# Light expert steps that fold gate and up apart, and a first gather whose second one-hot comes ahead of the splits

## Chip, core and metric

One core of a Trainium2 chip runs the whole program. The time is device time in microseconds (us) from the runs of the compiled program; the trace is one execution by the hardware profiler. Engines: PE is TensorE (matmuls), PEld its weight loads, DVE VectorE, ACT ScalarE, SP the queue that issues nearly all DMAs.

## What is computed

A two-layer decoder trunk on 256 tokens of width 1024, in float32. The first layer is FoX attention and a dense SwiGLU, the second a Griffin recurrent block and a mixture of eight SwiGLU experts, of which each token uses two. After each channel mixer a gated per-layer embedding is added. The change lies in the experts:

```python
def _moe_swiglu(x, w_router, b_router, w_gu, w_down):        # cut
    logits = xt @ w_router + b_router
    top_logit, top_idx = lax.top_k(logits, 2)
    top_w = softmax(top_logit)
    # tokens sorted by expert, and for each expert e:
    gate, up = split(xs @ w_gu[e], 2)                        # (n, 1024) @ (1024, 2 * 3584)
    y = (silu(gate) * up) @ w_down[e]                        # (n, 3584) @ (3584, 1024)
    out = zeros.at[row_tok].add(y * row_w)
```

## The kernel before

Every float32 matrix is cut into two parts of reduced precision, `hi` (a cast on ACT, L131) and `lo` (the rest, a subtraction on DVE, L132); a product is the sum of hi-hi, hi-lo and lo-hi matmuls. The weights are streamed: the class `Stream` holds a list of 1 MiB chunks, loads them ahead on SP's queue into whatever room is free, and splits them, two pieces to a chunk. Split pieces lie in four buffers each for `whi` and `wlo`, so a split can run only as far ahead as TensorE has finished with the piece four places earlier. `take()` hands out the next chunk and starts loads and splits (`ahead()`).

The router (`route_logits`, `route`) finds each token's two experts, and for each token its place (`posm`) in its experts' lists; `pos_ps`, a PSUM bank of the kind `mm` (there are two of them), holds the counts. `rank()` orders the experts by their number of tokens on the chip, since the five fullest ("heavy", up to 128 tokens) and the three emptiest ("light", up to 64) are treated differently. It reads the counts in `pos_ps` through `cnt_ps`. The first place is fixed, so the first gather doesn't need the ranking.

`gather(i)` makes one one-hot matrix for each half of the tokens (`one_hots`), multiplies the tokens by them on TensorE (L1059), and evacuates the four banks into `xe` (L1061).

An expert's 3584 inner columns are worked off in 7 steps of 512, and heavy and light steps of different experts take turns (`expert_steps`): 35 heavy and 21 light steps, each light step followed by a heavy one. Within a step s the program has the gate product in two halves (`moe_gu_half`), the transposition of the hidden tile of the step before (`moe_h_transpose`), the first half of the up product, the down product of the step before (`moe_down`), and the second half of the up product (`moe_up`). For a heavy step a product of gate or up has 24 matmuls of 512 columns, and the down product 24. For a light step the 64 tokens' hi and lo parts lie side by side in 128 columns, so that gate, up and down have 16 each. The two halves of the result must then be added: this is the fold, a matmul with the matrix `fold` that also transposes (L1113), four for the gate and four for the up product (each runs as two matmuls in the trace). Ahead of it ACT copies the products from PSUM (L1087, L1096). Behind it come Silu on ACT (L1115), the product on DVE (L1116), the cast on ACT (L1118) and the difference on DVE (L1119), whose result `z` is the operand of the light step's down product (L1131, L1132).

The program is written in this order, but a scheduling layer decides the order of each engine's queue from it when the program is built; `tc.issue_after(x)` keeps what is traced in it behind x on x's engine. Each engine then works its own queue in order.

Of the kernel before, what the change touches and what calls it, by code (L numbers as in the profile page):

```python
# [7 lines left out]
F32 = mybir.dt.float32  # L8
# [49 lines left out]
class Stream:  # L58


    def __init__(self, nc, pool, slab):
        self.nc, self.pool, self.slab = nc, pool, slab
        self.todo, self.raws, self.parts = [], [], []
        self.used = 0
        self.limit = None
        self.lent, self.extra = {}, {}
        self.n_raw, self.n_slab, self.where = N_RAW, 0, []

# [48 lines left out]
    def _split_one(self, alloc=None):  # L117
        nc, n = self.nc, len(self.parts)
        i, q = divmod(n, 2)
        _, _, split, (m, width) = self.todo[i]  # L120
        if not split:
            self.parts.append(None)
            return
        shape = [P, m // 2, width]
        if alloc is None:
            hi = self.pool.tile(shape, F32R, tag="whi", name=f"whi{n}", bufs=N_PIECE)
            lo = self.pool.tile(shape, F32R, tag="wlo", name=f"wlo{n}", bufs=N_PIECE)
        else:
            hi, lo = alloc(shape, F32R), alloc(shape, F32R)
        piece = self.raws[i][q]  # L130
        nc.scalar.copy(hi, piece)  # L131
        nc.vector.tensor_sub(lo, piece, hi.bitcast(F32))  # L132
        self.parts.append((hi, lo))
        if q:
            self.raws[i] = None

    def ahead(self):
        n = len(self.todo)
        while len(self.raws) < n:
            waiting = self.where[self.used + N_PIECE // 2:]  # L140
            free = [w for w in self.extra if w not in waiting]
            if len(self.raws) in self.lent:
                self._load_one()
            elif free:
                self._load_one(free[0])
            elif waiting.count("raw") < self.n_raw:
                self._load_one()
            elif waiting.count("slab") < self.n_slab:
                self._load_one("slab")
            else:  # L150
                break
        upto = min(2 * n, 2 * self.used + max(N_PIECE, 2))
        if self.limit is not None:
            upto = min(upto, max(self.limit, 2 * self.used + 2))
        while len(self.parts) < upto:
            self._split_one()

    def take_raw(self):
# [22 lines left out]
def hybrid_trunk_kernel(ctx: ExitStack, tc: tile.TileContext, x, p, ln_mix_g, ln_mix_b, ln_ffn_g, ln_ffn_b,  # L181
# [171 lines left out]
    def splits_after(*ins):  # L353

        with ExitStack() as st:
            for i in ins:
                st.enter_context(tc.issue_after(i.ins))
            ws.limit = None
            ws.ahead()

    def transposed(get, tb, dst):
# [597 lines left out]
    def route(tb, lg_ps):  # L959
# [14 lines left out]
        if tb:  # L974
            T.matmul(o, ones_b, sel[:, 0, :], start=True, stop=False)
        T.matmul(o, before, sel[:, tb, :], start=tb == 0, stop=True)
        posm_i.append(V.scalar_tensor_tensor(posm[:, tb, :], o, 1.0, self32[:, tb, :], op0=ALU.add, op1=ALU.mult))

        def weights():
            w1, w2 = small("w1", 1), small("w2", 1)  # L980
# [9 lines left out]
    def split_x3(tb, *after):  # L990
        t = [slab([P, D], F32R) for _ in range(2)]
        with ExitStack() as st:
            for i in after:
                st.enter_context(tc.issue_after(i.ins))
            A.copy(t[0], x3[tb])
            V.tensor_sub(t[1], x3[tb], t[0].bitcast(F32))
        return t

    pos_ps = bank("mm")
    wts, lgs, evac, x3s, posm_i = [], [], [], [], []  # L1000
    for tb in range(NT):
        row_chunks(accs[tb], parts, tb, False, True, tb == 1)
        t, ins = residual_norm(accs[tb], x2[tb], "mix1")
        x3.append(t)
        if tb:
            steps = ple_proj(pT, lambda: slab([P, D]))
            for _ in range(3):
                ple, last = next(steps)
            with tc.issue_after(last.ins):
                lgs.append(route_logits(1))  # L1010
            x3s.append(split_x3(1, *evac[2:]))
            with tc.issue_after(lgs[1][1].ins):
                wts.append(route(0, lgs[0][0]))
            with tc.issue_after(lgs[1][2].ins):
                next(steps)
            wts.append(route(1, lgs[1][0]))
            splits_after(posm_i[1])
        else:
            lgs.append(route_logits(0))
            x3s.append(split_x3(0, *evac))  # L1020
# [11 lines left out]
    def one_hots(at, pos, i):  # L1032

        oh = mp.tile([P, NT, CAP], F32R, tag="oh", name=nm("oh"), bufs=1)
        for tb in range(NT):
            V.tensor_scalar(oh[:, tb, :].rearrange("p (h s) -> p h s", h=at.shape[1]), at, pos[:, tb, i:i + 1], None, op0=ALU.is_equal)
        return oh

    def gather(i):


        small = i >= N_BIG
        cap = CAP_S if small else CAP
        oh = one_hots(slots1[:, None, 0:cap].to_broadcast([P, CAP // cap, cap]), posr if i else posm, i)
        if small:
            xe = slab([P, KD, 2, CAP_S], F32R)
            to = xe
# [4 lines left out]
        for n, d0 in enumerate(range(0, KD, nd)):  # L1052
            b = bank(("tr", "mm")[n % 2])
            bv = b.rearrange("p (d l s) -> p d l s", d=nd, l=2)
            for d in range(nd):
                c = slice((d0 + d) * P, (d0 + d + 1) * P)
                for part in range(2):
                    for tb in range(NT):
                        T.matmul(bv[:, d, part, :], x3s[tb][part][:, c], oh[:, tb, 0:cap],  # L1059
                                 start=tb == 0, stop=tb == NT - 1)  # L1060
            (V.tensor_copy if i == 0 and n % 2 else A.copy)(to[:, d0:d0 + nd, :, :], bv)  # L1061
        b = bank("tr")
        br = b.bitcast(F32R)
        for tb in range(NT):
            T.transpose(br[:, TOK[tb]], oh[:, tb, :], ident_r)
        ohT = mp.tile([P, S], F32R, tag="ohT", name=nm("ohT"), bufs=3)
        return xe, ohT, A.copy(ohT, b[:, 0:S])

    def moe_gu_half(i, o, k0):
        xe = placed[i][0]  # L1070
# [19 lines left out]
    def moe_up(i, ub, g):  # L1090
# [5 lines left out]
        A.copy(g[1], ub)  # L1096
        return g

    def moe_h_transpose(i, h, last=False):
        b = bank("tr")  # L1100
        t = aux([P, 2, 4, P], F32R, tag="y") if last else z_tile(0, (P, 2, 4, P), F32R)
        if i < N_BIG:
            for k in range(4):
                T.transpose(b[:, k * P:(k + 1) * P], h[:, k * P:(k + 1) * P], ident)
            hT, hTl = t[:, 0, :, :], t[:, 1, :, :]
# [1 line left out]
            A.copy(hT, bv)  # L1107
            V.tensor_sub(hTl, bv, hT.bitcast(F32))
            return hT, hTl
        bv = b.rearrange("p (u k t) -> p u k t", u=2, k=4)  # L1110
        for u in range(2):
            for k in range(4):
                T.matmul(bv[:, u, k, :], h[u][:, k * P:(k + 1) * P], fold, start=True, stop=True)  # L1113
        f = mp.tile([P, 512], F32, tag="sl", name=nm("sl"), bufs=1)[:, 0:256].rearrange("p (k t) -> p k t", k=4)
        A.activation(f, bv[:, 0, :, :], AF.Silu)  # L1115
        V.tensor_mul(f, f, bv[:, 1, :, :])  # L1116
        hT = t[:, 0, :, :]
        A.copy(hT[:, :, 0:CAP_S], f)  # L1118
        V.tensor_sub(hT[:, :, CAP_S:], f, hT[:, :, 0:CAP_S].bitcast(F32))  # L1119
# [99 lines left out]
                        late_expert(lt, big, e)  # L1219

    placed = {0: gather(0)}
    ws.room(N_RAW - 2, 4)
    cnt_ps = pos_ps[:, 32:32 + N_EXP]
    for tb in range(NT):
# [23 lines left out]
                V.tensor_mul(t, perm, by_expert[:, tb, None, :].to_broadcast([P, N_EXP, N_EXP]))  # L1248
                V.tensor_reduce(by_place[:, tb, :], t, axis=AX.X, op=ALU.add)

    with tc.issue_after(placed[0][2].ins):
        for w in wts:
            w()
        rank()
# [3 lines left out]
    for s in range(LAST + 1):  # L1258
# [18 lines left out]
            more["x"] = lambda: [x_tile() for _ in range(2)]  # L1277
        if s == LATE_STEP - 8:
            ws.room(N_RAW - 2, 3)
        if s < LAST:  # L1280
            gb = bank("mm")
            moe_gu_half(i, gb, 0)
            moe_gu_half(i, gb, 4)
        if s:
            hT = moe_h_transpose(pi, h, s == LAST)
        if s < LAST:
            g = moe_gate_out(i, gb)
            ub = bank("mm")
            moe_gu_half(i, ub, 0)
        if s == LAST - 1:  # L1290
            h_next = moe_up(i, ub, g)
        if s + 1 < LAST and STEPS[s + 1][1] == 0:
# [65 lines left out]
```

## Time and profile before

| | us |
|---|---|
| median of 3 runs | 1505.9 |
| lowest and highest run | 1501.11, 1506.09 |
| profiled execution, time | 1506.23 |
| profiled execution, span of the trace | 1504.5 |

| engine | busy us | share of the span |
|---|---|---|
| PE | 1434.0 | 95% |
| PEld | 1216.3 | 81% |
| DVE | 1217.9 | 81% |
| ACT | 1020.5 | 68% |

The expert steps begin at about 490 us of the span and end at about 1460. The queue of the 16 DMA engines is 80.6% busy over the span. A share of busy time is an average over stages with different limits, and two instructions of an engine may overlap in the trace; so what a stage is worth is read from the waits and from the order of time in it. TensorE's clock has two levels, 1.2 and 2.4 GHz; the trace gives the granted share, 1.00 or 0.50, and its mean over the span is 0.984.

### The profile page before, as it was taken

The numbers are of one execution on the slowest core, as the hardware profiler recorded it, in microseconds if no ns is written. First come the engines' busy times: TensorE is split into PE (matmuls) and PEld (weight loads), VectorE is DVE, ScalarE is ACT, GpSimd is POOL, SyncE is SP. The second block draws the span as 40 slices with busy tenths as digits, with TensorE's granted clock in tenths as the row PEclk, the third lists the DMA queues.
The fourth block names the chain that finished last, engine by engine and source line by source line (L and its number), as shares of the span: only waits on it lengthen the run. The fifth ranks groups of instructions, "written<-read, shape, count | busy, mean of one in ns | idle before, by whom it ended". The sixth has DMA issues, their size and how long they took to land. (4 is left out here: it accounts for less than half of the span.)

```text
span 1504.5 us, 21794 instructions
## 1 busy us (share of the span) xinstructions
PE 1434.0 (95%) x7820; PEld 1216.3 (81%) x7820; DVE 1217.9 (81%) x1382; ACT 1020.5 (68%) x1251; POOL 36.6 (2%) x44
## 2 busy tenths in 40 slices
PE   8999999999998999999999998999999999999987
PEld 7997999989986887777778776777777777787767
DVE  6568355577787889989988988898998888898996
ACT  4545344454663778878787876887786877887863
POOL 4000000000210000000000000000000000000000
PEclk9999999999998999999999999999999999999999
DMA  9635555565474689999999998999999999999950
GB/s 323 203 131 192 180 195 197 180 213 176 155 279 167 245 309 331 396 345 385 393 377 364 332 338 338 372 389 384 336 376 336 340 363 351 349 391 370 374 188 29
DMA packets 219285, 439.71 MB, mean 292 GB/s; under 512 B 11570, under 2 KB 68258, under 8 KB 219170
## 3 DMA queue, kind: packets, MB, share of 16 engines
q1 hardware_dynamic: 219138, 438.26, 80.6%
q8 instruction: 63, 1.03, 0.3%
q14 instruction: 52, 0.43, 0.1%
q10 hardware_dynamic: 32, 0.00, 0.0%
HBM read 437.14 MB, written 1.05 MB: 291 GB/s over the span
## 5 line engine op out<-in xcount | busy, mean ns | idle before, releaser
L132 DVE TENSOR_TENSOR wlo<-raw,whi 128x1024 fp32r<-128x1024 f32 x523 | 624.7, 1225 | 118.7 <-ACT whi L131 107.3
L131 ACT CAST whi<-raw 128x1024 fp32r<-128x1024 f32 x523 | 536.6, 1051 | 160.5 <-PE acc L382 62.1
L132 DVE TENSOR_TENSOR wlo<-slab,whi 128x1024 fp32r<-128x1024 f32 x220 | 261.6, 1221 | 30.7 <-ACT whi L131 28.6
L131 ACT CAST whi<-slab 128x1024 fp32r<-128x1024 f32 x220 | 226.5, 1051 | 49.0 <-PE mm L382 23.2
L380 PE MATMUL mm<-whi,xe 128*128 128x512 f32 x560 | 223.3, 399 | 0.1
L381 PE MATMUL mm<-wlo,xe 128*128 128x512 f32 x560 | 221.5, 395 | 2.1 <-DVE wlo L132 2.0
L382 PE MATMUL mm<-whi,xe 128*128 128x512 f32 x560 | 219.8, 393 | 0.0
L1078 PE MATMUL mm<-whi,slab 128*128 128x512 f32 x336 | 134.5, 402 | 5.4 <-issue 4.3
L1079 PE MATMUL mm<-wlo,slab 128*128 128x512 f32 x336 | 136.0, 407 | 0.8 <-DVE wlo L132 0.8
L380 PE MATMUL mm<-slab,whi 128*128 128x256 f32 x480 | 136.5, 284 | 0.0
L382 PE MATMUL mm<-slab,wlo 128*128 128x256 f32 x480 | 135.8, 283 | 0.0
L381 PE MATMUL mm<-slab,whi 128*128 128x256 f32 x480 | 135.8, 283 | 0.0
L381 PE MATMUL acc<-wlo,z 128*128 128x512 f32 x336 | 134.0, 399 | 0.4 <-DVE wlo L132 0.3
L382 PE MATMUL acc<-whi,z 128*128 128x512 f32 x336 | 132.3, 394 | 0.0
L381 PEld LDWEIGHTS mm<-wlo,xe 128*128 128x128 f32 x560 | 106.3, 190 | 26.7 <-DVE wlo L132 5.8
L380 PE MATMUL acc<-whi,z 128*128 128x512 f32 x336 | 125.2, 395 | 0.7 <-ACT z L1107 0.7
L382 PEld LDWEIGHTS mm<-whi,xe 128*128 128x128 f32 x560 | 106.0, 189 | 22.4
L380 PEld LDWEIGHTS mm<-whi,xe 128*128 128x128 f32 x560 | 106.2, 190 | 21.6 <-ACT xe L1061 0.3
L380 PEld LDWEIGHTS mm<-slab,whi 128*128 128x128 f32 x480 | 92.1, 192 | 0.5
L381 PEld LDWEIGHTS mm<-slab,whi 128*128 128x128 f32 x480 | 92.1, 192 | 0.4
L382 PEld LDWEIGHTS mm<-slab,wlo 128*128 128x128 f32 x480 | 92.1, 192 | 0.0
L1131 PE MATMUL acc<-whi,z 128*128 128x512 f32 x168 | 65.2, 408 | 20.4 <-DVE z L1119 20.4
(302 smaller groups left out, 2267.7 us busy)
## 6 DMA issues: line engine op xcount, KB each, us to landing
raw<-in_moe_w_gu_dram SPq DMA_DIRECT2D x133, 1024.0 KB
slab<-in_moe_w_gu_dram SPq DMA_DIRECT2D x144, 512.0 KB
raw<-in_moe_w_down_dram SPq DMA_DIRECT2D x62, 1024.0 KB
slab<-in_moe_w_down_dram SPq DMA_DIRECT2D x74, 512.0 KB
raw<-in_ffn_w_gu_dram SPq DMA_DIRECT2D x22, 1024.0 KB
x<-in_moe_w_gu_dram SPq DMA_DIRECT2D x36, 512.0 KB
raw<-in_fox_w_in_dram SPq DMA_DIRECT2D x11, 1024.0 KB
raw<-in_ffn_w_down_dram SPq DMA_DIRECT2D x11, 1024.0 KB
```

Of the source, the lines that this page charges most:

```text
L131: nc.scalar.copy(hi, piece)
L132: nc.vector.tensor_sub(lo, piece, hi.bitcast(F32))
L380: T.matmul(o, lh, rh, start=first, stop=False)
L381: T.matmul(o, lh, rl, start=False, stop=False)
L382: return T.matmul(o, ll, rh, start=False, stop=last)
L1078: T.matmul(o, both, hi, start=k == 0, stop=False)
L1079: T.matmul(o, both, lo, start=False, stop=k == KD - 1)
L1131: T.matmul(y[n], h, hi[:, HALF[n]], start=first, stop=False)
```

## The change

Two places are changed.

First, the light steps. `moe_gate_fold` is new: behind the first half of a light step's own up product it folds the gate product and applies Silu to it, into a tile of its own (`slT`; before, the tile `sl` of the heavy steps was used). `moe_h_transpose` folds only the up product for a light step, then multiplies, casts and subtracts as before. It is traced between the two halves of the next step's gate product, where before it stood behind both.

Second, the first gather. `ws.hold` keeps the stream from splitting while the router runs. The splits are then traced behind the second one-hot of the first gather (`oh_i`), and the weights of the tokens and `rank()` behind the last of these splits (`ws.last_split`, on DVE) instead of behind the copy `ohT` (on ACT). `route(1)` is traced behind the difference of the second half of the tokens (`lo3`). All four evacuations of the first gather are ACT copies; before, two of them were DVE's.

```diff
@@ Stream
-        nc.vector.tensor_sub(lo, piece, hi.bitcast(F32))
+        self.last_split = nc.vector.tensor_sub(lo, piece, hi.bitcast(F32))
...
-        while len(self.parts) < upto:
+        while len(self.parts) < upto and not self.hold:
             self._split_one()
@@ router
+    ws.hold = True
     pos_ps = bank("mm")
...
-            wts.append(route(1, lgs[1][0]))
-            splits_after(posm_i[1])
+            with tc.issue_after(lo3[1].ins):
+                wts.append(route(1, lgs[1][0]))
@@ gather
-            (V.tensor_copy if i == 0 and n % 2 else A.copy)(to[:, d0:d0 + nd, :, :], bv)
+            A.copy(to[:, d0:d0 + nd, :, :], bv)
...
-        return xe, ohT, A.copy(ohT, b[:, 0:S])
+        A.copy(ohT, b[:, 0:S])
+        return xe, ohT, oh_i
@@ light steps
+    def folded(h):
+        bv = bank("tr")[:, 0:256].rearrange("p (k t) -> p k t", k=4)
+        for k in range(4):
+            T.matmul(bv[:, k, :], h[:, k * P:(k + 1) * P], fold, start=True, stop=True)
+        return bv
+
+    def moe_gate_fold(g):
+        f = mp.tile([P, 4, CAP_S], F32, tag="slT", name=nm("slT"), bufs=1)
+        A.activation(f, folded(g[0]), AF.Silu)
+        return f, g[1]
...
-        bv = b.rearrange("p (u k t) -> p u k t", u=2, k=4)
-        for u in range(2):
-            for k in range(4):
-                T.matmul(bv[:, u, k, :], h[u][:, k * P:(k + 1) * P], fold, start=True, stop=True)
-        f = mp.tile([P, 512], F32, tag="sl", name=nm("sl"), bufs=1)[:, 0:256].rearrange("p (k t) -> p k t", k=4)
-        A.activation(f, bv[:, 0, :, :], AF.Silu)
-        V.tensor_mul(f, f, bv[:, 1, :, :])
+        f, u = h
+        V.tensor_mul(f, f, folded(u))
@@ before the steps
     placed = {0: gather(0)}
+    splits_after(placed[0][2])
+    split_i = ws.last_split
...
-    with tc.issue_after(placed[0][2].ins):
+    with tc.issue_after(split_i.ins):
         for w in wts:
             w()
         rank()
@@ steps
+        early = s and pi >= N_BIG
         if s < LAST:
             gb = bank("mm")
             moe_gu_half(i, gb, 0)
+        if early:
+            hT = moe_h_transpose(pi, h, s == LAST)
+        if s < LAST:
             moe_gu_half(i, gb, 4)
-        if s:
+        if s and not early:
             hT = moe_h_transpose(pi, h, s == LAST)
...
             moe_gu_half(i, ub, 0)
+            if i >= N_BIG:
+                g = moe_gate_fold(g)
```

What the scheduling layer makes of it, at three places. First TensorE in the heavy step behind the second light one. Before, the up folds (`tr` from `fold`) stand behind the whole gate product `mm_5935`, ahead of the up product `mm_5999`:

```order
L380 MATMUL mm_5935<-whi_5942,xe_4845 128x512
L381 MATMUL mm_5935<-wlo_5943,xe_4845 128x512
L382 MATMUL mm_5935<-whi_5942,xe_4845 128x512
L1113 MATMUL tr_5982<-fold,z_5847 128x64 x4
L380 MATMUL mm_5999<-whi_5962,xe_4845 128x512
```

Now they stand in the middle of the gate product, `mm_5943`, after its second piece of four:

```order
L380 MATMUL mm_5943<-whi_5930,xe_4829 128x512
L381 MATMUL mm_5943<-wlo_5931,xe_4829 128x512
L382 MATMUL mm_5943<-whi_5930,xe_4829 128x512
L1105 MATMUL tr_5967<-fold,z_5848 128x64 x4
L380 MATMUL mm_5943<-whi_5946,xe_4829 128x512
```

The up folds moved forward by twelve matmuls of 512 columns; the gate's folds of this light step were already hoisted by the layer before.

Second, ACT in the light step just before that. Before, the copy of the gate product (L1087) is followed by the hidden cast of the heavy step (L1107), and the Silu of the light step only comes fifteen rows later, with the product's cast right behind it; around that place the queue reads:

```order
L131 CAST whi_6004<-slab_5756 128x1024
L131 CAST whi_6008<-slab_5757 128x1024
L1115 ACTIVATE sl_5992<-tr_5982 128x256
L131 CAST whi_6026<-raw_5776 128x1024
L1118 CAST z_5983<-sl_5992 128x4x64
L131 CAST whi_6030<-raw_5776 128x1024
```

Now the Silu (L1110) follows the copy of the gate product (L1089) within the light step, and two casts of weight pieces stand ahead of that copy:

```order
L131 CAST whi_5853<-raw_5611 128x1024
L131 CAST whi_5857<-raw_5611 128x1024
L1089 COPY z_5848<-mm_5803 128x512
L131 CAST whi_5878<-raw_5633 128x1024
L131 CAST whi_5882<-raw_5633 128x1024
L1110 ACTIVATE slT_5869<-tr_5870 128x256
```

The Silu moved from the following heavy step into the light step itself; the cast of the product (L1127) stays in the heavy step.

Third, DVE at the first gather. Before, four splits lie between the second `posm` (places of the tokens) and the second one-hot `oh`, and the ranking begins behind it:

```order
L977 SCALAR_TENSOR_TENSOR posm<-mm_4627,self_4623 128x8
L132 TENSOR_TENSOR wlo_4810<-z_4192,whi_4809 128x1024
L132 TENSOR_TENSOR wlo_4814<-z_4193,whi_4813 128x1024
L132 TENSOR_TENSOR wlo_4818<-raw_4258,whi_4817 128x1024
L132 TENSOR_TENSOR wlo_4822<-raw_4258,whi_4821 128x1024
L1036 TENSOR_SCALAR oh_4842<-slots_95,posm 128x128
L1232 TENSOR_TENSOR rank_4836<-rank_4836,slots 128x8
L1233 SCALAR_TENSOR_TENSOR key<-mm_4627,rank_4836 128x8
```

Now the one-hot follows `posm`, and the splits and then the ranking follow it:

```order
L977 SCALAR_TENSOR_TENSOR posm<-mm_4627,self_4623 128x8
L1037 TENSOR_SCALAR oh_4826<-slots_95,posm 128x128
L132 TENSOR_TENSOR wlo_4876<-z_4192,whi_4875 128x1024
L132 TENSOR_TENSOR wlo_4880<-z_4193,whi_4879 128x1024
L132 TENSOR_TENSOR wlo_4884<-raw_4258,whi_4883 128x1024
L132 TENSOR_TENSOR wlo_4888<-raw_4258,whi_4887 128x1024
L981 TENSOR_TENSOR w_312_4894<-mx_4772 128x1
L981 TENSOR_TENSOR w_314_4903<-mx_4792 128x1
L1241 TENSOR_TENSOR fold<-ident_r 128x64
L1242 TENSOR_SCALAR rank_4818<-slots 128x8
L1243 TENSOR_TENSOR rank_4818<-rank_4818,slots 128x8
L1244 SCALAR_TENSOR_TENSOR key<-mm_4627,rank_4818 128x8
```

The one-hot moved ahead of four splits, and the readers of `pos_ps` (`mm_4627`) moved behind them. On TensorE the first gate product (`mm_4938`) waits for DVE, now as before; the row of the new order, with what it waits for, between its neighbours:

```order
L1060 MATMUL mm_4860<-oh_4826,slab_4766 128x128
L1060 MATMUL mm_4860<-oh_4826,slab_4689 128x128
L1060 MATMUL mm_4860<-oh_4826,slab_4767 128x128
L1066 MATMUL tr_4870<-ident_r,oh_4826 128x128 x2
L380 MATMUL mm_4938<-whi_4875,xe_4829 128x512 [waits DVE_49]
L381 MATMUL mm_4938<-wlo_4876,xe_4829 128x512
```

Before, the operation waited for was DVE's evacuation of the gather's second bank (L1061); now DVE evacuates none, and it is the last reader of `pos_ps`, the second `key` (L1252), eleven rows of DVE's queue behind the first (L1244).

## Rows read from the trace of the kernel before

**Rows 1.** Waits of PE, 580 to 1470 us: us in total, times, longest.
```profile
PE acc L1131 <- DVE z L1119: 20.4, 14, 2.7
PE tr L1113 <- ACT z L1087: 1.1, 2, 0.7
```

**Rows 2.** PE in order of time: start, us, line, operation, idle before and releaser.
```profile
609.83 1.00 PE L1113 MATMUL tr<-fold,z 128*128 128x64 f32 x8
...
613.26 0.39 PE L382 MATMUL mm<-whi,xe 128*128 128x512 f32 x1
615.01 0.50 PE L1131 MATMUL acc<-whi,z 128*128 128x512 f32 x1 [1.36 <-DVE z L1119]
615.34 0.39 PE L1132 MATMUL acc<-wlo,z 128*128 128x512 f32 x1
```

**Rows 3.** DVE in order of time, the same heavy step.
```profile
612.25 0.41 DVE L1116 TENSOR_TENSOR sl<-sl,tr 128x256 f32<-128x256 f32 x1
613.39 1.23 DVE L132 TENSOR_TENSOR wlo<-raw,whi 128x1024 fp32r<-128x1024 f32 x1 [0.72 <-ACT whi L131]
614.53 0.42 DVE L1119 TENSOR_TENSOR z<-sl,z 128x256 fp32r<-128x256 f32 x1
```

**Rows 4.** ACT in order of time, three casts in the light step before, then this step.
```profile
591.23 2.95 ACT L131 CAST whi<-raw 128x1024 fp32r<-128x1024 f32 x3
...
610.98 0.38 ACT L1115 ACTIVATE sl<-tr 128x256 f32<-128x256 f32 x1
...
613.26 0.40 ACT L1118 CAST z<-sl 128x256 fp32r<-128x256 f32 x1
```

**Rows 5.** The longest wait on PE, and the stretch behind it (columns in rows 8).
```profile
750.91 0.80 PE L1131 MATMUL acc<-whi,z 128*128 128x512 f32 x1 [2.73 <-DVE z L1119]
...
750.70:754.10 3.40, 3.19 (x8) 2.52 (x9) 0.58 (x2) 1.64 (x2) 0.00 (x0) 0.50 1.05 393
```

**Rows 6.** DVE in order of time, first gather.
```profile
478.19 0.17 DVE L977 SCALAR_TENSOR_TENSOR posm<-mm,self 128x8 f32<-128x8 f32 x1
478.27 2.35 DVE L132 TENSOR_TENSOR wlo<-z,whi 128x1024 fp32r<-128x1024 f32 x2
480.54 2.35 DVE L132 TENSOR_TENSOR wlo<-raw,whi 128x1024 fp32r<-128x1024 f32 x2
482.81 0.28 DVE L1036 TENSOR_SCALAR oh<-slots,posm 128x128 fp32r<-128x128 f32 x1
483.01 0.16 DVE L1232 TENSOR_TENSOR rank<-rank,slots 128x8 f32<-128x8 f32 x1
...
484.95 0.16 DVE L1241 TENSOR_TENSOR key<-mm,caps 128x8 f32<-128x8 f32 x1
```

**Rows 7.** PE in order of time, first gather and first gate matmul.
```profile
477.59 0.45 PE L1059 MATMUL tr<-oh,slab 128*128 128x128 f32 x2 [0.37 <-DVE oh L1036]
...
483.15 1.76 PE L1059 MATMUL tr<-oh,slab 128*128 128x128 f32 x7 [4.54 <-DVE oh L1036]
...
489.65 0.76 PE L380 MATMUL mm<-whi,xe 128*128 128x512 f32 x1
```

**Rows 8.** Light, heavy, heavy step: us, PE, PEld, DVE, ACT, POOL busy, clock, DMA, GB/s.
```profile
590.07:604.39 14.32, 14.32 (x70) 11.73 (x68) 14.32 (x15) 12.61 (x14) 0.00 (x0) 1.00 0.96 326
604.39:621.49 17.10, 15.74 (x74) 12.83 (x72) 15.22 (x15) 14.18 (x17) 0.00 (x0) 1.00 1.04 398
621.49:638.27 16.78, 16.78 (x77) 13.91 (x76) 15.84 (x16) 13.53 (x14) 0.00 (x0) 1.00 1.04 394
```

**Rows 9.** Stretches around the start of the first gate product, same columns.
```profile
481.05:484.46 3.41, 1.31 (x6) 1.31 (x7) 3.13 (x11) 0.00 (x0) 0.00 (x0) 0.50 0.11 16
...
491.29:494.71 3.42, 3.42 (x9) 2.65 (x9) 2.35 (x12) 1.64 (x4) 0.00 (x0) 0.50 0.00 0
```

**Rows 10.** A busy stretch of DMA, same columns; transfers over 580 to 1400 us.
```profile
690.80:724.70 33.90, 32.54 (x150) 26.72 (x149) 31.04 (x30) 27.67 (x31) 0.00 (x0) 1.00 1.04 394
...
DMA packets 127015, 297.04 MB, mean 362 GB/s; under 512 B 6367, under 2 KB 6367, under 8 KB 126950
```

More of the change, by code (lines that the diff above doesn't have):

```diff
@@ L64, in __init__ @@
         self.used = 0
-        self.limit = None
+        self.limit, self.hold = None, False
         self.lent, self.extra = {}, {}
@@ L357, in splits_after @@
                 st.enter_context(tc.issue_after(i.ins))
-            ws.limit = None
+            ws.limit, ws.hold = None, False
             ws.ahead()
@@ L976, in route @@
         T.matmul(o, before, sel[:, tb, :], start=tb == 0, stop=True)
-        posm_i.append(V.scalar_tensor_tensor(posm[:, tb, :], o, 1.0, self32[:, tb, :], op0=ALU.add, op1=ALU.mult))
+        V.scalar_tensor_tensor(posm[:, tb, :], o, 1.0, self32[:, tb, :], op0=ALU.add, op1=ALU.mult)
         def weights():
@@ L995, in split_x3 @@
             A.copy(t[0], x3[tb])
-            V.tensor_sub(t[1], x3[tb], t[0].bitcast(F32))
+            lo3.append(V.tensor_sub(t[1], x3[tb], t[0].bitcast(F32)))
         return t
+    ws.hold = True
     pos_ps = bank("mm")
-    wts, lgs, evac, x3s, posm_i = [], [], [], [], []
+    wts, lgs, evac, x3s, lo3 = [], [], [], [], []
     for tb in range(NT):
@@ L1035, in one_hots @@
         for tb in range(NT):
-            V.tensor_scalar(oh[:, tb, :].rearrange("p (h s) -> p h s", h=at.shape[1]), at, pos[:, tb, i:i + 1], None, op0=ALU.is_equal)
-        return oh
+            oh_i = V.tensor_scalar(oh[:, tb, :].rearrange("p (h s) -> p h s", h=at.shape[1]), at, pos[:, tb, i:i + 1], None, op0=ALU.is_equal)
+        return oh, oh_i
     def gather(i):
@@ L1043, in gather @@
         cap = CAP_S if small else CAP
-        oh = one_hots(slots1[:, None, 0:cap].to_broadcast([P, CAP // cap, cap]), posr if i else posm, i)
+        oh, oh_i = one_hots(slots1[:, None, 0:cap].to_broadcast([P, CAP // cap, cap]), posr if i else posm, i)
         if small:
@@ L1097, in moe_up @@
         return g
+    def folded(h):
[7 more added lines that the diff above has]
+        return f, g[1]
     def moe_h_transpose(i, h, last=False):
-        b = bank("tr")
         t = aux([P, 2, 4, P], F32R, tag="y") if last else z_tile(0, (P, 2, 4, P), F32R)
         if i < N_BIG:
+            b = bank("tr")
             for k in range(4):
```

## Prediction

> **What bounds the kernel now.** I read the page's busy shares first (PE 95%, DVE 81%, ACT 68%, in the table above): TensorE is the bound, so a change pays for the TensorE time that it frees and for nothing else. Then the waits, over the expert steps only. One of them stands far above the rest: the down product of a light step (L1131) waits for the low half of its hidden tile (`z`, L1119), 14 times, 20.4 us; the longest is 2.73 us [rows 1]. Next I looked at one of these in the order of time on the three engines [rows 2 to 4]. TensorE ends the eight folds at 610.83, issues the first half of the up product (its last matmul at 613.26) and then stands until 615.01. In this time four dependent operations run, alternately on ACT and DVE, and each stands in line behind a weight split: Silu 610.98, product 612.25, cast 613.26, difference 614.53 to 614.95. The chain takes 4.12 us from the last fold; twelve matmuls at the pitch of 0.227 us cover 2.72.
>
> Idle time understates the loss, since a matmul's shown end lies behind the next one's earliest start. Start to start, 613.26 to 615.01 is 1.75 us where 0.227 would do, and the next interval is 0.33 instead of 0.227 [rows 2]: 1.52 + 0.10 = 1.62 us lost with each short wait. Thirteen are like it (20.4 - 2.73 = 17.7 = 13 x 1.36). The fourteenth, at 750.91, is one split longer, so it loses 3.0, and the clock is 0.50 (1.2 GHz) for the 3.4 us behind it [rows 5].
>
> The second place is the gather of the first expert. TensorE starts it at 477.59 and then has nothing until 483.15, because DVE has put four splits, 478.27 to 482.89, between `posm` and the second one-hot [rows 6, 7].
>
> **Part one: gate and up folded apart.** The number of instructions is the same: eight folds, one Silu, one product, one cast, one difference for each light step. What moves is where they stand. The Silu leaves the closing chain, as the gate's four folds now stand behind the first half of the same step's up product. The up folds stand between the two halves of the next gate product (the excerpt above), so 24 matmuls, 5.45 us, lie between the last fold and the down product instead of 12, 2.72 us. The new chain: the DVE product waits for at most one split (1.22), takes 0.41; the ACT cast waits for at most one cast (1.05), takes 0.40; the difference waits for at most one split, takes 0.42 [rows 3, 4]. That is 4.7 us at worst, under 5.45. The wait goes; if the cover were gone the chain would cost up to 4.7 - 2.7 = 2.0 us again.
>
> What is late next is DVE. A light step at 590.07 has DVE busy for 14.32 of 14.32 us; the heavy step behind it 15.22 of 17.10 [rows 8]. The pair takes 31.42, DVE works 29.54 of it, TensorE needs 31.42 - 1.62 = 29.80. So the two engines are nearly level. Upper end of the gain: 1.62 for each pair. Lower end: DVE still waits once for an ACT cast, 0.72 us as at 613.39 [rows 3], which makes 29.54 + 0.72 = 30.26, a gain of 1.16. I take 1.2, near the lower end, since splits and matmuls rarely mesh without loss. The sum is 13 x 1.2 = 15.6, and 2.5 for the long wait (3.0 less the same 0.4): **18.1 us**, between 17.6 and 24.
>
> The half clock behind the long wait: eight matmul intervals of 0.43 instead of 0.227, **1.6 us**. It follows that wait and none of the short ones I looked at, so I take it as gone; at worst it stays.
>
> New waits. A fold of the gate needs the ACT copy of the gate product. In the excerpt two splits stand in front of that copy, the second of which needs the buffer of the gate's last weight piece. So from the gate's end: 0.20 until ACT may start, 0.95 for the cast at ACT's pitch (three in 2.95) [rows 4], 0.58 for the copy, together 1.7 us. Nine matmuls, 2.04 us, stand between, so here it is covered. Counting the program's order, 14 of the 21 light steps have 1.1 to 2.3 us between, and seven have 0.9 or less, where five had so little before; of those five, two waited, 1.1 us in all [rows 1]. Two more such places cost about 0.55 each: **-1.0 us**, between 0 and -6 (seven times 0.8). The copy of the up product comes earlier against its fold than the bound (2.72 us, one cast in front): nothing.
>
> **Part two: the first gather.** The second one-hot now stands right behind `posm`: start near 478.40, end near 478.7, and TensorE goes on at 478.7 instead of 483.15. But what is gained in the gather isn't gained behind it. The gate product's output bank is the one in which `pos_ps` lies, which the ranking reads until its second `key` (L1252 of the new kernel); the new order shows the first gate matmul waiting for DVE. On DVE that `key` stands behind the one-hot, the four splits and the ranking's first half. By the old durations: splits 478.6 to 483.15 (twice 2.27), two differences and the fold 0.35, first rank step 483.6. From the rank step at 483.01 to the end of `key` at 485.11 it was 2.10 us [rows 6]; two more small operations (L983, L984) make 2.35: 486.0. So the gate product starts at 486.0 instead of 489.65 [rows 7]. The clock was at half there until 494.71, so that 12 matmuls ran at half pitch [rows 9]; TensorE will stand again before 486.0, so I let the same 12 run at half: **3.5 us**. Ends: 2 if the ranking drags, 5 if the clock is up earlier. The two copies that move from DVE to ACT, and the table load now ahead of the third copy on ACT, end before 486 or within the first half of the gate product: nothing. No DMA moves on SP's queue, since the raw buffers come free by the same splits, some 4 us earlier.
>
> **Sum.** 18.1 + 1.6 - 1.0 + 3.5 = 22.2. The profiled execution took 1506.23 us, its span 1504.5, so 1.7 us lie outside and stay. That is 0.3 above the median of 1505.9, within their spread, so I correct nothing: 1506.2 - 22.2 = **1484.0 us**.
>
> **Rivals.**
> *The transfers become the bound* (1495 us). A step loads six chunks of 1 MiB, 6.29 MB. Two pairs and one heavy step take 2 x 31.42 + 16.78 = 79.6 us now [rows 8], and 31.46 MB in it are 395 GB/s, which is just what busy stretches show: 394 and 398 [rows 8, 10]. After the change they would have to take 77 us, 408 GB/s. For it: no stretch I saw goes much above 398. Against it: the queue runs ahead while gathers and combines hold TensorE up, and no split in the list of waits waits for a landing. If the head start covers half, half of part one's 18 us stays away with the clock's 1.6: 1506.2 - 3.5 - 9 + 1 = 1495.
>
> The Trainium skill, "DMA: Bandwidth & Descriptors", section on where 436 GB/s comes from, would have this rival decide by itself: it says that transfers from HBM into SBUF are held to about 358 GB/s for a core. By that rule the expert steps, at 362 GB/s on average over 820 us [rows 10], have no room left, and removing waits would bring nothing there: 1506.2 - 3.5 = 1502.7, from the gather alone. The trace disagrees with 394 GB/s over 33.9 us [rows 10], and I go by the trace.
>
> *The chain still ends last* (1502 us). The splits queue up differently and the difference still comes after the up product's half; part two alone is left, 1506.2 - 3.5 = 1502.7. Against it: 4.7 against 5.45 at the worst.
>
> *Slower: the gate folds wait in all 21 light steps* (1519 us). If ACT reaches the two splits in front of the copy only at the gate's end, with the heavy step's hidden cast (0.58) ahead of them, the copy ends 0.20 + 0.58 + 2 x 0.95 + 0.57 = 3.25 us behind the gate; a cover of 1.5 on average leaves 1.75 x 21 = 37 us, less the 24 gained: 1519. It decides from (22.2 + 1.0) / 21 = 1.1 us a fold. Against it: the first of the two needs a piece freed four matmuls earlier, and ACT is idle 1.7 us in such a step (12.61 of 14.32) [rows 8].
>
> *All of it comes back* (1476 us): 24 + 1.6 + 5.
>
> **How the numbers follow.** About 0.5%, 7.5 us, is what a measurement of this kernel tells from no change. Chances: forecast 0.61 (1478 to 1491), transfers or DVE hold back half 0.21 (1491 to 1499), chain still last 0.06 (1500 to 1504), slower 0.04, all back 0.08. To hold 8 in 10, the range takes the forecast, most of the second case and half of the last: 1476 to 1497. Faster by over 0.5% are the first, most of the second and the last: 0.87; within 0.5% 0.09; slower 0.04.
>
> **What the new profile would show.** Right: the down product's wait for `z` is gone from TensorE's waits, pairs of steps take 30.0 to 30.4 us, DVE is over 96% busy in them, the first gate matmul starts 3 to 4 us earlier, the 750 us dip is gone. Wrong: splits that wait for landings at 394 GB/s; TensorE waiting for low halves (`wlo`) in light steps; folds of the gate waiting for the ACT copy by more than 1 us each; the ranking's `key` later than 487.

## The result, and the profile after

| | us |
|---|---|
| median of 4 runs | 1480.86 |
| lowest and highest run | 1479.26, 1483.78 |
| profiled execution, time | 1481.4 |
| profiled execution, span | 1479.6 |
| ratio to before, 95% interval | 0.9838 [0.9806, 0.9869] |

A second set of five runs (`c1_changed` below) has the median 1481.93 and again the ratio 0.9838, [0.9813, 0.9863]. So the change takes about 24 us, 22 were forecast, and the range 1476 to 1497 holds it.

TensorE's waits in the expert steps (560 to 1450 us: us in total, times, longest), the profile after:

```profile
PE mm L1080 <- issue: 6.7, 1, 6.7
PE tr L1118 <- DVE sl L1096: 6.6, 7, 1.6
...
PE mm L381 <- DVE wlo L132: 5.0, 10, 1.4
...
PE mm L1081 <- DVE wlo L132: 1.8, 3, 0.8
...
PE tr L1105 <- ACT z L1089: 1.1, 2, 0.7
```

The wait for `z` that led the list [rows 1] is gone, and no wait of the light step's down product (now L1140) has come in its place. The gate folds wait as before, 1.1 us in all. What has grown is the wait for low halves, in light steps (L1081) too; the same two lines in the profile before, where 1079 is the line that is now 1081:

```profile
PE mm L381 <- DVE wlo L132: 2.0, 6, 0.5
...
PE mm L1079 <- DVE wlo L132: 0.8, 1, 0.8
```

The chain itself, in the heavy step that follows the second light one (the counterpart of [rows 2 to 4]), on TensorE, DVE and ACT:

```profile
600.81 1.00 PE L1105 MATMUL tr<-fold,z 128*128 128x64 f32 x8
607.19 0.39 PE L1140 MATMUL acc<-whi,z 128*128 128x512 f32 x1
...
601.85 0.42 DVE L1125 TENSOR_TENSOR slT<-slT,tr 128x256 f32<-128x256 f32 x1 [0.53 <-PE tr L1105]
602.18 1.22 DVE L132 TENSOR_TENSOR wlo<-slab,whi 128x1024 fp32r<-128x1024 f32 x1
603.32 0.42 DVE L1128 TENSOR_TENSOR z<-slT,z 128x256 fp32r<-128x256 f32 x1
...
602.30 0.41 ACT L1127 CAST z<-slT 128x256 fp32r<-128x256 f32 x1 [0.24 <-DVE slT L1125]
```

From the end of the folds, 601.81, to the end of the difference, 603.74, it is 1.93 us (4.12 before), and the down product comes 5.38 us behind the folds (4.18 before, 1.36 of it idle). DVE now waits for the folds (0.53 us), where before the down product waited for DVE. The pair of steps (columns as in [rows 8]) takes 14.59 + 15.48 = 30.07 us where it took 31.42, TensorE has no idle time in it, and DVE is busy for 29.31 us:

```profile
583.50:598.09 14.59, 14.59 (x69) 11.78 (x68) 14.59 (x15) 12.82 (x15) 0.00 (x0) 1.00 1.01 372
598.09:613.57 15.48, 15.48 (x73) 12.84 (x72) 14.72 (x15) 13.70 (x16) 0.00 (x0) 1.00 1.04 395
```

The first gather, on DVE and TensorE (counterparts of [rows 6, 7]):

```profile
476.28 0.17 DVE L977 SCALAR_TENSOR_TENSOR posm<-mm,self 128x8 f32<-128x8 f32 x1 [0.18 <-PE mm L976]
476.48 0.29 DVE L1037 TENSOR_SCALAR oh<-slots,posm 128x128 fp32r<-128x128 f32 x1
...
483.72 0.14 DVE L1252 TENSOR_TENSOR key<-mm,caps 128x8 f32<-128x8 f32 x1
...
476.82 1.00 PE L1060 MATMUL tr<-oh,slab 128*128 128x128 f32 x7
...
480.22 0.33 PE L1066 MATMUL tr<-ident_r,oh 128*128 128x128 f32 x2
483.92 0.79 PE L380 MATMUL mm<-whi,xe 128*128 128x512 f32 x1 [3.36 <-DVE key L1252]
```

The one-hot stands right behind `posm`, the gather ends at 480.55, and TensorE then waits 3.36 us for the second `key`, as the prediction read from the new order.

### The profile page after: what moved, and what is told of

It reads as the page before. It is cut to its first block, busy times and chain, and to the rows that moved or that the text cites. A ratio compares the mean times of both kernels' runs of the same rounds, so it can differ in the third digit from the quotient of the medians.

```text
span 1479.6 us, 21774 instructions
## 1 busy us (share of the span) xinstructions
PE 1426.9 (96%) x7820; PEld 1209.5 (82%) x7820; DVE 1211.7 (82%) x1380; ACT 1019.6 (69%) x1253; POOL 36.7 (2%) x44
## 5 line engine op out<-in xcount | busy, mean ns | idle before, releaser
L381 PE MATMUL mm<-wlo,xe 128*128 128x512 f32 x560 | 221.4, 395 | 5.1 <-DVE wlo L132 5.0
L1081 PE MATMUL mm<-wlo,slab 128*128 128x512 f32 x336 | 136.0, 407 | 1.9 <-DVE wlo L132 1.8
L381 PE MATMUL mm<-slab,whi 128*128 128x256 f32 x480 | 135.8, 283 | 0.0
L381 PE MATMUL acc<-wlo,z 128*128 128x512 f32 x336 | 133.1, 396 | 0.2 <-DVE wlo L132 0.2
L381 PEld LDWEIGHTS mm<-wlo,xe 128*128 128x128 f32 x560 | 106.1, 189 | 32.0 <-DVE wlo L132 11.0
L382 PE MATMUL acc<-whi,z 128*128 128x512 f32 x336 | 132.0, 393 | 0.0
L380 PE MATMUL acc<-whi,z 128*128 128x512 f32 x336 | 126.1, 399 | 0.7 <-ACT z L1121 0.7
L381 PEld LDWEIGHTS mm<-slab,whi 128*128 128x128 f32 x480 | 92.1, 192 | 0.4
L1081 PEld LDWEIGHTS mm<-wlo,slab 128*128 128x128 f32 x336 | 64.1, 191 | 21.9 <-DVE wlo L132 7.9
```

Of the source, the lines that this page charges most:

```text
L380: T.matmul(o, lh, rh, start=first, stop=False)
L381: T.matmul(o, lh, rl, start=False, stop=False)
L382: return T.matmul(o, ll, rh, start=False, stop=last)
L1081: T.matmul(o, both, lo, start=False, stop=k == KD - 1)
```

## Experiments

**The two parts apart.** Part one alone (`e1_light_only`) keeps the light steps of the change and gives the gather back its old order:

```diff
-            with tc.issue_after(lo3[1].ins):
-                wts.append(route(1, lgs[1][0]))
+            wts.append(route(1, lgs[1][0]))
+            splits_after(posm_i[1])
...
-    with tc.issue_after(split_i.ins):
+    with tc.issue_after(placed[0][2].ins):
```

> Part one alone: the light steps fold gate and up apart as in the changed kernel, the first gather is that of the kernel before. Theory (the two parts add, each worth what the two traces show up to and behind the start of step 1: 24.9 us in all, 6.7 of it ahead of step 1): 1506 - 18.2 = 1488 us; TensorE has no wait for the light z; the first gate product starts near 489.6; the half clock at 750 us is gone; from step 1 to the end the times are those of the changed kernel. Rival (the transfers hold back part of the gain once the head start of the first gather is missing): 1492 to 1500 us, splits waiting for landings behind 600 us.

Measured: 1483.48 us, ratio 0.9861 [0.9839, 0.9882], span 1480.9. No wait for the light `z`; the first gate product starts 11.45 us behind the second `posm`, as before. The gain is larger than expected, and no transfer holds it back: ACT's waits for landings are 0.9 us in all (560 to 1450 us). Of the span's 23.5 us, 3.0 are there before step 1, 2.9 of them ahead of the second `posm` and so by no edit; part one gives 20.5 from step 1 on.

Part two alone (`e2_gather_only`) has the light steps of before:

```diff
-        early = s and pi >= N_BIG
+        early = False
...
-            if i >= N_BIG:
-                g = moe_gate_fold(g)
```

> Part two alone: the first gather of the changed kernel, the light steps of the kernel before. Theory: first gate matmul near 484 to 486 instead of 489.65, step 1 starts 4.5 to 6.7 us earlier, all of it kept to the end, 14 waits for z of 20 us in all as before: 1499 to 1502 us. Of the 6.7 us that the changed kernel gained up to step 1, 1.9 were there before the second one-hot, since the 3.4 us of half clock at 474 us were missing. If that is chance from one execution to the next, it is missing or there here regardless of the edit, and the gain from posm on is 4.8; if it follows from the edit, the half clock at 474 is missing here too. Rival (the earlier start only moves the wait to a transfer or a split in steps 1 to 4): 1504 to 1506 us.

Measured: 1498.5 us, ratio 0.9958 [0.9944, 0.9973], span 1497.8; the first gate product 7.65 us behind the second `posm`. By the median that is more than the gather. TensorE's wait for `z` (560 to 1450 us), and the place where the long wait [rows 5] was:

```profile
PE acc L1145 <- DVE z L1133: 18.2, 14, 1.4
...
741.64 0.50 PE L1145 MATMUL acc<-whi,z 128*128 128x512 f32 x1 [0.53 <-DVE z L1133]
```

Fourteen waits still, but the long one has shrunk from 2.73 to 0.53 us and no half clock follows it; the step there takes 16.31 us instead of 19.97, and the next one gives 2.0 back. So that wait and its half clock go with either part. What this brings doesn't last here: near 925 us the half clock is 3.4 us longer than before, near 1048 us 3.4 us of it are new, and behind the start of step 1 the trace is 0.2 us longer than the one before. By the medians the two gains (21.6 and 6.6 us, against 24 together) seem not to add up. Counted from the second `posm` to the end they do: 1026.3 us before, 1005.6 with part one, 1022.7 with part two, 1002.1 (`c1_changed`) and 1003.4 (first trace) with both. That is 20.6 and 3.6, and together 24.1 or 22.9.

**Which half of part one does it?** `e3_gate_early_only` leaves the gate fold and Silu early and puts the up fold back behind both gate halves (`early = False` alone).

> The changed kernel, but the up fold of a light step stands behind both halves of the next gate product, as before: only the gate's fold and Silu are taken out of the closing chain, and the cover is 12 matmuls (2.72 us) instead of 24. Theory (cover against chain): the chain without Silu is 4.12 - 1.2 = 2.9 us in a typical step and up to 4.7, so the wait for z stays in most of the 14 light-to-heavy places at 0.1 to 1.4 us each: 1483 to 1497 us, 1488 taken. Rival (the Silu alone made the chain too long): no wait for z on TensorE, 1481 us like the changed kernel.

Measured: 1484.64 us, ratio 0.9856 [0.983, 0.9883]. By the waits the rival holds: one for `z`, of 0.3 us, is left. The time is above the rival's 1481; of the 3.8 us by which the trace is longer than that of `c1_changed` from step 1 on, 2.6 arise in the last combine (below), at half clock. In the step looked at before, TensorE and DVE:

```profile
605.30 1.00 PE L1105 MATMUL tr<-fold,z 128*128 128x64 f32 x8
608.96 0.39 PE L1140 MATMUL acc<-whi,z 128*128 128x512 f32 x1
...
608.21 0.42 DVE L1128 TENSOR_TENSOR z<-slT,z 128x256 fp32r<-128x256 f32 x1
```

The folds end at 606.30, the difference at 608.63, and the down product starts at 608.96: 2.33 us of chain in 2.66 of cover (the time for which TensorE has other work). Taking the Silu away was enough, with 0.33 us to spare here.

`e4_place_only` does the other half: both folds and the Silu together, at the early place.

```diff
-        f, u = h
+        f, u = moe_gate_fold(h)
...
-            if i >= N_BIG:
-                g = moe_gate_fold(g)
```

> The changed kernel, but gate and up are folded together again, with the Silu behind them, at the new early place between the halves of the next gate product: the place is changed, the folding apart is undone. Theory (cover against chain): the chain with Silu is 4.12 us in a typical step, 5.7 at the worst with one cast more in front, the cover 24 matmuls or 5.45 us, so the wait for z is gone or nearly: at most 0.3 us in a few places, 1480 to 1484 us. Then the place alone does the work and the folding apart adds nothing that can be measured. Rival (the Silu has to leave the chain too): the wait for z stays in most places by 0.5 us or more, 1488 us or above.

Measured: 1486.75 us, ratio 0.9872 [0.9844, 0.9899], between the two expectations, and no wait for `z`. The order on the chip shows that the edit did less than meant: in all but five steps the scheduling layer had hoisted the gate fold and its Silu again. In one of the five (16 matmuls in a row), TensorE and DVE:

```profile
653.85 1.89 PE L1105 MATMUL tr<-fold,z 128*128 128x64 f32 x16
661.12 0.39 PE L1140 MATMUL acc<-whi,z 128*128 128x512 f32 x1
...
659.45 0.42 DVE L1128 TENSOR_TENSOR z<-slT,z 128x256 fp32r<-128x256 f32 x1
```

Folds to difference: 655.74 to 659.87, 4.13 us, the old chain; the cover is 5.38. So in those five places the place alone is enough; for the others that isn't shown. Where each stood alone, either half took the wait away; together they leave over 3 us of slack. The 6 us above the changed kernel were tested again on one chip, with the changed kernel itself:

> The changed kernel once more, unaltered, as the control for the two that follow on the same chip. Theory (whether a short wait is followed by half clock is chance from one execution to the next): the gather from the second posm to the first gate matmul takes 7.6 us as before, the steps have the same waits as in the first execution of this kernel, but the half-clock stretches lie elsewhere or are more than its 31 us between 400 and 1480 us; median 1480 to 1484 us. Rival (they belong to the program): the same stretches at 541, 920, 1040 and 1446 us, and only these.

> Gate and up folded together at the early place, once more, beside the changed kernel on the same chip. Theory (place alone is enough, and the 6 us above the changed kernel came from 51 us of half clock against 31): within 3 us of the changed kernel here, no wait for z on TensorE. Rival (folding apart is worth 4 to 6 us by itself): again 4 to 6 us above the changed kernel of the same call.

Measured: `c1_changed` 1481.93, `c2_place_only` 1484.37, ratio 0.9865 [0.9837, 0.9892]. The difference is now 2.4 us; all four runs of `c2_place_only` (1483.48 us and more) lie above all five of `c1_changed` (1482.27 and less). From the start of step 1 to that of the last light step the two traces differ by 0.4 us; 3.1 us arise behind it, most of them in the last combine (the products that add the experts' results, L1161), where both have a wait of the same size and one has half clock behind it. TensorE's wait, and the stretch behind it, in `c2_place_only` and then in the first trace of the changed kernel:

```profile
1429.24 0.50 PE L1161 MATMUL acc<-y,ohT 128*128 128x512 f32 x1 [2.14 <-DVE y L1153]
...
1431.10:1438.00 6.90, 6.22 (x15) 4.22 (x15) 5.27 (x7) 1.63 (x2) 0.00 (x0) 0.51 0.00 0
```

```profile
1429.56 0.50 PE L1161 MATMUL acc<-y,ohT 128*128 128x512 f32 x1 [2.13 <-DVE y L1153]
...
1431.50:1438.30 6.80, 6.12 (x26) 4.54 (x25) 6.61 (x8) 2.70 (x3) 0.00 (x0) 1.00 0.00 0
```

There `c1_changed` stays at 1.00 too. That folding apart is worth something in the light steps beyond the place is therefore not shown.

`c1_changed` itself came out as expected: the gather takes 7.64 us, the waits in the steps are the same, and half clock adds up to 37.5 us between 400 and 1480 us, where it was 31. But the rival has a part in it: that at 920, 1040 and 1446 us comes again, that at 541 us (6.8 us) is shorter and later (3.4 at 545), and around the first gather it is 13.7 us instead of 3.4.

**What is late next: the bank of the first gather.** `e5_rank_first` puts the ranking up to the second `key` ahead of the four splits; `e6_counts_out` copies the counts out of the bank at once and keeps the splits' place:

```diff
+    with tc.issue_after(placed[0][2].ins):
+        cnt_i = V.tensor_copy(cnts, cnt_ps)
+    splits_after(cnt_i)
...
-        V.scalar_tensor_tensor(key, cnt_ps, 8.0, rank0, op0=ALU.mult, op1=ALU.add)
+        V.scalar_tensor_tensor(key, cnts, 8.0, rank0, op0=ALU.mult, op1=ALU.add)
```

> The changed kernel, but behind the second one-hot of the first gather the ranking goes first, up to the second key (the last reader of the bank that the first gate product needs), then the four splits, then the rest. Theory (the gate product waits for the bank, not for the gather): in the changed kernel TensorE stood 3.36 us at 480.6 for that key. Here the key ends some 2.3 us behind the one-hot, before TensorE has ended the gather, so the first gate matmul starts 0 to 0.5 us behind the last transposition of the gather, if the first split is there: 2 to 3.4 us earlier, counted from the second posm on: 1477 to 1480 us. Rival (what is late next takes it back: the first low half, or an evacuation on ACT behind the table load): the start moves by less than 1 us, and the time stays at 1481.

> The changed kernel, but DVE copies the eight counts out of the bank right behind the second one-hot, and the ranking reads the copy: the bank is free at once, and the splits keep their place ahead of the ranking. Theory: one small operation more on DVE (about 0.16 us), the first gate matmul starts right behind the gather, 3 to 3.4 us earlier than in the changed kernel counted from the second posm on, and its first low half is there in time, since the splits begin 0.2 us later than before: 1476.5 to 1479 us. Rival (an evacuation of the gather on ACT, behind the table load, is what the gate product waits for next): start earlier by under 1.5 us, 1479 to 1481 us.

> The counts copied out of the bank, once more, beside the changed kernel on the same chip. Theory: 0 to 2 us below the changed kernel of the same call, as the start of step 1 counted from the second posm came 1.85 us earlier, which is less than these runs can tell from nothing. Rival (the earlier start is lost again in the steps): 1 us or more above it.

Measured: 1482.73 us, ratio 0.986 [0.9839, 0.988]; 1481.98, 0.9852 [0.9832, 0.9872]; and beside `c1_changed` 1481.20, 0.9826 [0.9799, 0.9852]. The stretch from the second `posm` to the first gate matmul, in this order: before, after, `c1_changed`, `e5_rank_first`, `e6_counts_out`, `c3_counts_out` (the seventh column is the clock):

```profile
478.19:489.65 11.46, 6.82 (x35) 6.66 (x34) 7.91 (x26) 1.17 (x2) 0.00 (x0) 0.62 0.28 92
```

```profile
476.28:483.92 7.64, 4.05 (x34) 3.71 (x34) 7.29 (x26) 3.99 (x8) 0.00 (x0) 0.97 0.17 41
```

```profile
478.00:485.64 7.64, 5.50 (x35) 5.15 (x34) 7.29 (x26) 3.98 (x8) 0.00 (x0) 0.65 0.18 45
```

```profile
475.75:482.80 7.05, 6.92 (x35) 6.83 (x35) 6.63 (x21) 1.78 (x4) 0.00 (x0) 0.50 0.00 1
```

```profile
476.43:482.05 5.62, 5.40 (x35) 5.24 (x34) 5.55 (x12) 2.83 (x5) 0.00 (x0) 0.69 0.00 0
```

```profile
476.26:480.26 4.00, 3.78 (x34) 3.62 (x34) 3.96 (x7) 2.21 (x3) 0.00 (x0) 1.00 0.00 0
```

The wait for `key` is gone in all three, as expected; the times of the first two lie 2.7 and 3.0 us above the upper ends of what was expected. What is late next is TensorE's clock: at a mean clock of 0.50 and 0.69 the gather itself fills much of the time saved (7.05 and 5.62 us), at 1.00 it takes 4.00. Where the clock is up, DVE is late: in `c3_counts_out` TensorE waits for a low half before step 1:

```profile
487.41 0.50 PE L381 MATMUL mm<-wlo,xe 128*128 128x512 f32 x1 [1.23 <-DVE wlo L132]
```

Even so its step 1 starts 4.4 us earlier than that of `c1_changed`, counted from the second `posm` (16.49 us behind it, not 20.93). Behind that start its trace is 5.7 us longer (those of `e5_rank_first` and `e6_counts_out` 5.8), although TensorE's waits are the same within 0.2 us: at 1142, 1347 and 1429 us its clock is 0.50, where `c1_changed` has 1.00 in the same places. So the trace bears out the rival, that the earlier start is lost again behind it; why the clock falls there is open. The median of `c3_counts_out`, 0.7 us below the changed kernel on the same chip, is within the spread: no version was shown to beat the changed kernel.

**How level are TensorE and DVE?** `e7_split_twice` does one difference of a weight piece twice for each light step:

```diff
         self.last_split = nc.vector.tensor_sub(lo, piece, hi.bitcast(F32))
+        if self.twice:
+            nc.vector.tensor_sub(lo, piece, hi.bitcast(F32))
+            self.twice = False
```

> The changed kernel with one difference of a weight piece done twice in each light step (21 times 1.15 to 1.2 us more on DVE, the same result, nothing else). Theory (TensorE and DVE are nearly level now: DVE is idle 0.8 us in a typical light-heavy pair): a typical pair grows from 30.07 by 1.2 - 0.8 = 0.4 us, TensorE waits for low halves (wlo) more often, 6 to 10 us over the 20 pairs: 1487 to 1491 us. Rival (TensorE alone is the bound and splits run far enough ahead): within 2 us of the changed kernel. Other rival (DVE alone is the bound): the whole 24 us, 1505 us.

Measured: 1491.04 us, ratio 0.9931 [0.9913, 0.9948]. The same pair of steps, and two of TensorE's waits (560 to 1460 us; L385 is L381 of the others, L133 and L135 are the differences):

```profile
581.93:596.73 14.80, 14.78 (x69) 11.54 (x68) 14.80 (x15) 12.98 (x16) 0.00 (x0) 1.00 1.02 370
596.73:612.78 16.05, 16.05 (x73) 12.75 (x72) 15.54 (x16) 13.55 (x16) 0.00 (x0) 1.00 1.04 396
...
PE mm L385 <- DVE wlo L133: 4.7, 9, 1.4
PE mm L385 <- DVE wlo L135: 2.9, 4, 1.8
```

The time is at the upper end of what was expected. The pair takes 30.85 us instead of 30.07: of 1.13 us more on DVE, 0.78 arrive at the end, though DVE was idle for 0.76. So less than half of that idle time could be used here. Over the whole run it is less: of 21 x 1.13 = 24 us, 9 to 14 arrive, by the medians or by the ratios. DVE is near its limit, but it isn't the bound in all steps, as the other rival (24 us) had it.

**Transfers.** `e8_one_ahead_less` lets the stream hold one raw buffer less in the expert steps (`N_RAW - 3` for `N_RAW - 2`).

> The changed kernel, but in the expert steps the stream may hold one raw buffer less (five instead of six beside the slabs), so that each load is issued later by one chunk of 1 MiB, some 2.6 us. Theory (the transfers are not the bound: no cast waits for a landing in the steps of the changed kernel): within 3 us of the changed kernel, 1479 to 1484 us. Rival (transfers nearly the bound at 390 GB/s): casts wait for landings, and the time rises by 8 us or more, 1489 us or above.

Measured: 1485.72 us, ratio 0.9895 [0.9878, 0.9913], between the two expectations. ACT's waits for landings (560 to 1450 us) are 3.7 us in all, four kinds of which this is the largest; in the changed kernel two kinds, 1.9 us:

```profile
ACT whi L131 <- DMA raw<-in_moe_w_gu_dram: 1.3, 4, 0.3
...
PE mm L1081 <- DVE wlo L132: 5.2, 10, 0.8
```

TensorE waits 3.4 us longer for low halves in light steps than in the changed kernel. So landings do not bound the steps, but there isn't a whole chunk of slack either. From the second `posm` to the end the trace is 4.2 us longer than that of `c1_changed`; 2.7 of these arise behind the wait in the last combine, with the clock at half there, so the steps lose little.

## Why the prediction was right, point by point

- **Part one, 18.1, with 1.6 for the half clock and -1.0 for the gate folds: 18.7 net.** Behind the start of step 1 the first trace after is 18.2 us shorter, `c1_changed` 20.3 and `e1_light_only` 20.5; the first holds 3.4 us more of half clock in step 3 than the others, which costs 1.6. The mechanism was right and the net size some 1.7 us low, but that hides larger errors that cancel; so much of it is luck. By steps, before against `c1_changed`:
- *The short waits, 13 x 1.2 = 15.6.* In nine of the 13 pairs neither trace has half clock: they gain 14.0 us, 1.56 each on average (1.35 in the pair shown, 1.95 at most), nearly all of the 1.62 that was idle. In the pair shown, of the 0.76 that DVE is idle only 0.23 is a wait for a cast, where I charged 0.72; the rest is the wait for the folds. The other four gain 8.3, with half clock in one trace or in both; in one of them the wait before the late experts (`issue`) is 6.7 us instead of 4.3.
- *The long wait, 2.5, and its half clock, 1.6.* Both went, but they brought 0.5, not 4.1. The two pairs, before and in the first trace after:

```profile
724.69:758.89 34.20, 31.47 (x142) 25.59 (x140) 29.86 (x28) 26.74 (x30) 0.00 (x0) 0.95 1.04 394
758.89:789.79 30.90, 30.71 (x142) 24.38 (x140) 28.85 (x28) 26.10 (x30) 0.00 (x0) 1.00 1.01 372
```

```profile
713.41:744.25 30.84, 30.68 (x141) 24.21 (x140) 27.19 (x26) 26.34 (x30) 0.00 (x0) 1.00 1.04 393
744.25:778.02 33.77, 32.00 (x142) 24.03 (x140) 31.08 (x30) 26.21 (x30) 0.00 (x0) 1.00 1.04 395
```

The pair with the wait is 3.36 us shorter, the pair behind it 2.87 longer: TensorE now waits in it for DVE, for `sl` and for low halves.

```profile
745.19 0.66 PE L1118 MATMUL tr<-ident_r,sl 128*128 128x128 f32 x4 [0.55 <-DVE sl L1096]
746.33 0.50 PE L1081 MATMUL mm<-wlo,slab 128*128 128x512 f32 x1 [0.48 <-DVE wlo L132]
...
751.47 0.50 PE L1081 MATMUL mm<-wlo,slab 128*128 128x512 f32 x1 [0.54 <-DVE wlo L132]
```

That pair takes 33.75 us in `e1_light_only` and 32.91 in `e2_gather_only` too, so it lies not with one part alone. The sum priced the wait where it stood and not the pair behind it. That `e2_gather_only` nearly loses the wait too may come from when the splits fall there, which an earlier start also moves; it was not shown.

- *The gate folds' new waits, 1.0,* didn't come: 1.1 us, 2 times, as before.
- *All other steps* lose 2.5 together, which the sum didn't hold. Step 48, the pair of 49 and 50, and step 55 with the last combine behind it (counted from 0) take 1.1 to 1.4 us more each, and in them TensorE now waits for DVE: 0.56 us for `sl` and 0.48, 1.36 and 1.36 us for a low half. The clock has a share in the rest, both ways.
- **Part two, 3.5.** The gate product starts 7.64 or 7.65 us behind the second `posm` in all eight traces with the new order as it is in the changed kernel, 11.46 and 11.45 with the old: 3.8 us, where the prediction's 486.0 for 489.65 is 3.65, rounded to 3.5. At step 1 it is 3.86 in `c1_changed`, where half clock lies as in the forecast, and 4.75 in the first trace after, where six matmuls ran at half pitch instead of twelve. That the bank, not the gather, would be late next was the right step.
- **Transfers become the bound: no.** 395 GB/s in the heavy step shown, 1.9 us of waits for landings, and `e1_light_only` keeps its gain without the gather's head start. By the rate the Trainium skill gives in "DMA: Bandwidth & Descriptors", in the section on where 436 GB/s comes from (about 358 GB/s), part one would have brought nothing; here too the trace disagrees, with 395 GB/s and 20.5 us gained by part one.
- **The chain still last: no.** 1.93 us in 5.38. My 4.7 was a bound for the worst meshing; either half of the edit was enough where it stood alone, so I had the margin too small.
- **DVE late next: yes.** It is seen in `wlo` on TensorE's list, in the pair behind the long wait and in `e7_split_twice`. But the prediction named waits for `wlo` in light steps as a sign of being wrong, and they came: 1.8 us, 3 times, for 0.8, once. It was no sign against the mechanism, since it follows from DVE being late next.
- **Not the edit's: 1.9 us of the first trace.** It started its second `posm` 1.9 us earlier. That isn't set by the edit: in `c1_changed`, the same program, it came at 478.00 again, and in the eight traces with the new order it lies anywhere from 475.14 to 478.21.

## What to carry to other kernels

When a short chain of dependent operations ends last behind an engine that is full, shortening the chain and moving it behind more independent work are two separate cures: measure each, since one may do. Then look at which engine is level with the one freed, and at the steps behind: here nearly all of a short wait came back (1.56 of 1.62 us a pair), but what the longest wait gave back was lost in the next pair, where that engine was late. Cost an edit from a fixed event just ahead of it, not from the start of the trace, or clock differences upstream will be booked as its gain; two parts that seemed not to add up by the medians did add up that way.

## What the runs showed of the hardware

Whether half clock follows a short wait differs between executions of one program. In step 20 TensorE waits 1.48 us for `sl` in both executions with gate and up at the early place, `e4_place_only` and then `c2_place_only`:

```profile
833.43 0.66 PE L1118 MATMUL tr<-ident_r,sl 128*128 128x128 f32 x4 [1.48 <-DVE sl L1096]
```

```profile
831.72 0.66 PE L1118 MATMUL tr<-ident_r,sl 128*128 128x128 f32 x4 [1.48 <-DVE sl L1096]
```

In the first the clock is 0.50 from 835.20 for 3.41 us, in the second it stays at 1.00. The copied counts ran the gather at 0.69 mean clock once and at 1.00 once. In the last combine, though, every program that was traced twice did the same twice. The wait there is 2.1 us in twelve of the thirteen traces, and the rest of the program behind it takes 49.9 to 50.2 us at full clock behind the wait (before, the changed kernel twice, `e1_light_only`, `e2_gather_only`) and 52.4 to 52.7 with half clock there (the other seven, among them `c2_place_only` and `e4_place_only`, `c3_counts_out` and `e6_counts_out`). So this part can belong to the program; what decides it was not found. The clock shows in the times: of the five runs of `c1_changed`, four at a mean clock of 0.987 took 1481.8 to 1482.3 us and one at 0.992 took 1477.55. Differences of 2 to 4 us between versions of this kernel are of that size, and are told from it only by tracing a stretch from an event to an event.
